# Placing the small matrix products of the norms in a three-block transformer kernel

## The chip, the cores and the metric

The kernel runs on one core of a Trainium2 chip. The metric is the device time of one execution in microseconds (us), smaller is better. The engines of the core are named as in the profile: PE is TensorE (matrix products, with PEld its weight loads), DVE is VectorE, ACT is ScalarE, POOL is GpSimd, SP issues most DMA transfers. Each engine works off its own instructions in the order in which they stand in its queue, and waits at one until what it needs has been signalled by the others.

## The reference

Three transformer blocks follow one another on one sequence of 512 tokens with 1024 features. The first block has a feed-forward network (FFN), a mixer of spatial gating and attention, and an FFN, all with norms that are modulated by a conditioning vector. The second has an FFN, a mixer with a recurrence and a convolution, and an FFN. The third has two layers of an attention mixer and an FFN. In the first two blocks every sub-layer has a norm ahead of it and another behind it; the third block has only the norms ahead, and a last one.

```
def rmsnorm(x, g):
    y = xf * lax.rsqrt(jnp.mean(xf * xf, axis=-1, keepdims=True) + RMS_EPS)
    return (y * g).astype(x.dtype)
def swiglu_2(x, w_gu, w_down):
    gu = x @ w_gu
    gate, up = gu[..., :D_FF], gu[..., D_FF:]
    return (jax.nn.silu(gate) * up) @ w_down
def second_block(...):
        f = swiglu_2(rmsnorm(x, ffn1_norm_pre[l]), ffn1_w_gu[l], ffn1_w_down[l])
        x = x + 0.5 * rmsnorm(f, ffn1_norm_post[l])
        m = hybrid_mixer_2(rmsnorm(x, mix_norm_pre[l]), w_in[l], ...)
        x = x + rmsnorm(m, mix_norm_post[l])
        f = swiglu_2(rmsnorm(x, ffn2_norm_pre[l]), ffn2_w_gu[l], ffn2_w_down[l])
        x = x + 0.5 * rmsnorm(f, ffn2_norm_post[l])
```

All inputs are float32, and D_FF is 2816.

## The kernel before

The sequence is cut into two halves of 256 tokens, half 0 and half 1. Activations lie with features on the partitions, as 8 tiles of 128 features x 256 tokens. Each half goes through the same phases: f10 (first FFN of the first block), m1 (its mixer), f11 (second FFN), f21, m2, f22 in the second block, m30, f30, m31, f31 in the third, and an end. The halves run side by side on the core, half 1 some microseconds behind half 0, so that one half's products can fill TensorE while the other half's norms and attention steps run on VectorE and ScalarE.

A large product is made of float16 parts: a float32 weight tile of 128 x 1024 arrives by DMA (`st`), ScalarE writes its high part (line 368) and VectorE its low part (line 369) into a slot `wr` of a ring of 12 slots (`RING`), and each 128 x 128 piece is used in three products with the high and low parts of the activations (`hh`). The slots are shared by the halves; a slot comes free when both halves have used it. An FFN has 22 tiles of gate and up products (`pgu`, 48 products each) and 8 tiles of down products (`po`, 66 products each); a mixer begins with projections (`pp`, 24 a tile) and ends with 8 `po` tiles of 24. All products go through one helper, so they all have line 320.

A norm is `rstd_bcast` (line 416) with what stands around it. The sum of squares of each token is collected in `acc` on ScalarE and VectorE (`sumsq`, line 434, for the norm ahead of a phase; lines 496 and 497 in `out_tiles` for the norm behind one). Two small float32 products with `ones`, called `nst`, put the sums on partitions; the trace has four records for them. VectorE makes the reciprocal root in small steps (line 421, and `rsqrt` from line 404) and a diagonal of it, `ndg` (line 426); the product `nbc` of ones with `ndg` (two records) spreads it over the partitions. Behind `nbc`, `prenorm` (line 454) scales and splits the 8 tiles of x into `hh` (lines 480, 446 to 450), which the next phase's products read; `postnorm` (line 473) scales the 8 tiles of the phase's output `y` and adds them to x. In the first two blocks a postnorm and the next prenorm of one half follow one another: nst, nbc, update of x and new squares, nst, nbc, `hh`.

What sets the order: the code gives every instruction a priority, and a scheduler makes each engine's fixed order from it when the kernel is built. The priority is the virtual time of the half (`vt[hf]`, which `adv` moves on with every tile of large products, plus `lag`, which is zero for half 0 and `LAGS[ph]`, 16 to 30 us, for half 1), times 200 a microsecond; a smaller number goes first. `boost(us)` moves what is written inside it ahead by so many virtual microseconds. All of a norm stands in `boost(BOOST["norm"])`, 80 us, so each of its steps goes to its engine's queue about as soon as its operands are there.

```
    def now(hf):
        tc.cur_priority = BASE + int((vt[hf] + lag[hf]) * PER_US)
    def boost(us=None):
        return tc.high_priority(int(us * PER_US))
```

Of the kernel before, what the change touches and what calls it, by code (L numbers as in the profile page):

```python
# [20 lines left out]
D = 1024  # L21
KD = 8
# [8 lines left out]
LATE = 6  # L31
WBS = {"m2_o": 0, "gu22": 0}
WB = 0
CB = 80
PB = 10
SEQ = ("G0 G1 G2 G3 K0 K1 K2 K3 U0 P0 U1 P1 C0 R0 R1 C1 R2 R3 B",
# [15 lines left out]
BASE = 2000000  # L52
PER_US = 200
# [195 lines left out]
def tile_three_blocks(ctx: ExitStack, tc: tile.TileContext, d, col_at, con_at, out, phases=None):  # L249
# [20 lines left out]
    vt = [0.0, 0.0]  # L270
    lag = [0.0, LAGS["f10"]]
# [5 lines left out]
# [4 lines that stand above are left out]
        us = CB if us is None else us  # L281
        return tc.high_priority(int(us * PER_US))
# [15 lines left out]
    def t1k(hf, shape=(128, TH), dt=F32, name="t"):  # L298
        return tmp.tile(list(shape), dt, name=name, tag=f"t{hf}")

    def b8k(hf, shape, dt, name):
        return big.tile(list(shape), dt, name=name, tag=f"b{hf}")
# [7 lines left out]
    def tiny(hf, n, name="n", dt=F32, p=128):  # L310
        return tin.tile([p, n], dt, name=name, tag=f"{name}{hf}")
# [4 lines left out]
    def psmall(hf, shape=(128, 512), dt=F32, name="pq"):  # L316
        return pss.tile(list(shape), dt, name=name, tag=f"sm{hf}")

    def mm(out_, l, r, start=True, stop=True):
        return PE.matmul(out_, lhsT=l, rhs=r, start=start, stop=stop, skip_group_check=True)  # L320
# [12 lines left out]
    ones = cons.tile([128, TH], F32, name="ones")  # L333
    V.memset(ones, 1.0)
    ones1 = ones[:, 0:128]
# [22 lines left out]
    class Weights:  # L358
# [3 lines left out]
        def slot(self, s):  # L362
            if s not in self.have:
                with boost(CB if self.name == "gu10" and s < 3 else WBS.get(self.name, WB)):
                    st = stage.tile([128, 1024], F32, name="st", tag="st")
# [38 lines left out]
    def rsqrt(hf, m, y, p=128):  # L404
        shape = list(m.shape)
        n = int(np.prod(shape[1:]))
        a = t1k(hf, name="rsa") if n > 8 else tin.tile([128, 8], F32, name="rsa", tag=f"rsa{hf}")
        a = a[:shape[0], :n]
        mi, yi = m.bitcast(I32), y.bitcast(I32)
        V.tensor_scalar(yi, mi, -0.5, float(0x5f3759df), op0=OP.mult, op1=OP.add)  # L410
        for _ in range(3):
            V.scalar_tensor_tensor(a, y, -0.5, m, op0=OP.mult, op1=OP.mult)
            V.tensor_tensor(a, a, y, op=OP.mult)
            V.scalar_tensor_tensor(y, a, 1.5, y, op0=OP.add, op1=OP.mult)

    def rstd_bcast(hf, acc, n, eps):
        st = psmall(hf, [128, 2, 2], name="nst")
        for j in range(2):
            mm(st[:, j], acc[:, j * 128:(j + 1) * 128], ones[:, 0:2], start=j == 0)
        m, y = tiny(hf, 2, "nm"), tiny(hf, 2, "ny")  # L420
        V.tensor_scalar(m, st[:, :, 0], 1.0 / n, eps, op0=OP.mult, op1=OP.add)
        rsqrt(hf, m, y)
        bc = psmall(hf, [128, TH], name="nbc")
        dg = tin.tile([128, TH], F32, name="ndg", tag=f"ndg{hf}", bufs=1)
        for j in range(2):
            V.tensor_scalar(dg[:, j * 128:(j + 1) * 128], ident, y[:, j:j + 1], None, op0=OP.mult)
        mm(bc, ones1, dg)
        return bc

    def sumsq(hf, src, n, scale=1.0):  # L430
        acc = t1k(hf, name="acc")
        for k in range(n):
            if k == 0:
                S.activation(acc, src(0), AF.Square, scale=scale)
            else:
                t = t1k(hf, name="sq")
                S.activation(t, src(k), AF.Square, scale=scale)  # L437
                V.tensor_tensor(acc, acc, t, op=OP.add)  # L438
        return acc

    def split(hf, hi, lo, src, scale_col=None, bias_col=None):
        if scale_col is not None:
            S.activation(hi, src, AF.Identity, scale=scale_col)
            V.scalar_tensor_tensor(lo, src, scale_col, hi, op0=OP.mult, op1=OP.subtract)
        elif bias_col is not None:
            S.activation(hi, src, AF.Identity, bias=bias_col)
            V.scalar_tensor_tensor(lo, src, bias_col, hi, op0=OP.add, op1=OP.subtract)
        else:
            S.activation(hi, src, AF.Copy)  # L449
            V.tensor_tensor(lo, src, hi, op=OP.subtract)  # L450

    first = {}

    def prenorm(hf, gcol, bcol=None, ph=None):
        if hf and ph:
            lag[1] = LAGS[ph]
        now(hf)
        with boost(BOOST["norm"]):
            x = xs[hf]
            bc = first.pop(hf, None)  # L460
            if bc is None:
                bc = rstd_bcast(hf, sumsq(hf, lambda k: x[:, k], KD), D, 1e-6)
            hh = b8k(hf, [128, 2, KD, TH], F16, "hh")
            for k in range(KD):
                t = t1k(hf, name="nh")
                V.scalar_tensor_tensor(t, x[:, k], gcol(k), bc, op0=OP.mult, op1=OP.mult)
                split(hf, hh[:, 0, k], hh[:, 1, k], t, bias_col=bcol(k) if bcol else None)
        return hh
# [4 lines left out]
    def postnorm(hf, acc, y, gcol):  # L473
        now(hf)
        with boost(BOOST["norm"]):
            bc = rstd_bcast(hf, acc, D, 1e-6)
            x = xs[hf]
            for k in range(KD):
                t = t1k(hf, name="nh")
                V.scalar_tensor_tensor(t, y(k), gcol(k), bc, op0=OP.mult, op1=OP.mult)  # L480
                V.tensor_tensor(x[:, k], x[:, k], t, op=OP.add)
# [32 lines left out]

    def ffn(hf, gu, dn, pre, bias, post, key):
        hh = prenorm(hf, pre, bias, key)
        acts = []
        for n in range(NF):
# [21 lines left out]
        def y(m):  # L540
            if not yb:
                yb[0] = b8k(hf, [128, KD, TH], F32, "y")
            return yb[0][:, m]
        acc = out_tiles(hf, W(dn), NF, x, y, AS / WS, key)
        postnorm(hf, acc, y, post)


# [191 lines left out]

    def mixer1(hf):  # L740
        hh = prenorm(hf, one_col(gpre, 8), one_col(mod, 24), "m1")
        px = pair(hh)
        if hf == 0:
# [127 lines left out]
        with boost(BOOST["mix"]):  # L871
            mix = b8k(hf, [128, 2, KD, TH], F16, "mix")
            bc = rstd_bcast(hf, sumsq(hf, ua, 4), 512, 1e-6)
            for k in range(4):
                t = t1k(hf, name="nh")
                V.scalar_tensor_tensor(t, ua(k), col("gna", k), bc, op0=OP.mult, op1=OP.mult)
                split(hf, mix[:, 0, k], mix[:, 1, k], t)
            for qt in range(2):
                to_channels(hf, ybs[qt], mix, 4, qt, lambda j: col("gnb", j))
        ys = [m2k(hf, [128, 2, TH], F32, "ym") for _ in range(4)]  # L880
        y = lambda m: ys[m // 2][:, m % 2]
        acc = out_tiles(hf, W("m1_o"), KD, pair(mix), y, 1.0 / WS)
        postnorm(hf, acc, y, one_col(gpost, 8))

    def row_rms(hf, y, n):
# [19 lines left out]

    def mixer2(hf):
        hh = prenorm(hf, lambda k: col("mpre2", k), None, "m2")
        px = pair(hh)
        if hf == 0:
# [361 lines left out]
        y = lambda m: ys[m // 2][:, m % 2]  # L1271
        acc = out_tiles(hf, W("m2_o"), KD, lambda k: (mix[:, k, 0], mix[:, k, 1]), y, 1.0 / WS)
        postnorm(hf, acc, y, lambda k: col("mpost2", k))


# [221 lines left out]
    for ph in phases:  # L1497
        if ph == "ada":
# [12 lines left out]
            for groups, key, n0, n1 in (((2, 3, 4), "f10", 2, NF), ((5, 6, 7), "f10", NF, NF + KD), ((8,), "f11", 2, NF)):  # L1511
                steps = [(g, k) for g in groups for k in range(8)]
                for i, (g, k) in enumerate(steps):
                    n = n0 + i * (n1 - n0) // len(steps)
# [28 lines left out]
```

## Time and profile before

| | us |
|---|---|
| three timed runs | 3427.9, 3428.2, 3434.75 |
| their median | 3428.2 |
| the profiled execution's own time | 3428.03 |
| its span in the trace | 3426.1 |
| TensorE busy in it | 3295.0 (96%) |
| VectorE busy | 2105.7 (61%) |
| ScalarE busy | 1372.9 (40%) |
| mean granted clock of TensorE | 0.983 of full speed |
| DMA queue of the weights, share of 16 engines | 30.9% |

A share of busy time is an average over all phases. A wait of TensorE is the time in which its next instruction stood at the head of its queue and an operand was missing; the view of the waits names the instruction that delivered it last. TensorE's clock has two levels, 2.4 GHz (granted clock 1) and 1.2 GHz (0.5), and the granted clock of a stretch is a mean over it.

### The profile page before, as it was taken

The page shows a single profiled execution, that of the slowest core. Times are in us where ns is not written, and L with a number is a line of the kernel's source. Part 1 is how long each engine was busy: PE and PEld are TensorE (multiplying, and loading weights), DVE is VectorE, ACT ScalarE, POOL GpSimd, SP SyncE. Part 2 cuts the span into 40 slices and gives each one's busy share as a digit, 9 for nine tenths or more (in the row PEclk, how much of TensorE's full clock was granted, in tenths as well). Part 3 has the DMA queues.
Part 4 walks back from the last instruction along what each step waited for, and adds up shares of the span by engine and source line. Part 5 has one row for each costly group of instructions (what it writes and reads, how often), then busy time and mean ns, then how long its engine had stood idle before and what let it go on. Part 6 is the DMA issues. An engine that isn't in the chain of part 4 may idle for free.

```text
span 3426.1 us, 71629 instructions
## 1 busy us (share of the span) xinstructions
PE 3295.0 (96%) x30113; PEld 2794.9 (82%) x30120; DVE 2105.7 (61%) x5012; ACT 1372.9 (40%) x2881; POOL 18.7 (1%) x24
## 2 busy tenths in 40 slices
PE   8999999999999999998879999999999999999998
PEld 5888867788888888886658888777888877778887
DVE  8952758844374436598894436996544379845443
ACT  4232356433243324434243334565433255553331
POOL 0000000000000000000000000000000000000000
PEclk9999999999999999997889999999999999999999
DMA  8932434233323333201022333332233343213331
GB/s 307 316 112 87 140 92 133 68 101 103 99 87 99 103 102 106 75 8 35 2 81 99 99 100 125 98 99 82 87 99 108 99 127 121 87 62 106 105 99 44
DMA packets 143603, 351.46 MB, mean 103 GB/s; under 512 B 16808, under 2 KB 58152, under 8 KB 143024
## 3 DMA queue, kind: packets, MB, share of 16 engines
q1 hardware_dynamic: 143280, 346.89, 30.9%
q8 instruction: 235, 3.85, 0.5%
q14 instruction: 88, 0.72, 0.1%
HBM read 334.24 MB, written 12.58 MB: 101 GB/s over the span
## 4 chain that ended last, share of the span: by engine, by line
PE 77%; DVE 15%; ACT 4%; issue 2%; DMA 2%; ACTq 0%; SPq 0%; DVEq 0%
PE pgu L320 38%; PE po L320 20%; PE pp L320 5%; PE ps L320 4%; DVE wr L369 2%; PE pt L320 2%; DVE mix L989 2%; PE ps L659 1%; ACT wr L368 1%; PE pT L320 1%; PE pxy L320 1%; PE pgl L320 1%; DVE acc L438 1%; PE pw L320 1%; DVE nh L480 1%
## 5 line engine op out<-in xcount | busy, mean ns | idle before, releaser
L320 PEld LDWEIGHTS <-wr 128*128 128x128 f16 x24000 | 2348.1, 98 | 326.5 <-issue 26.5
L320 PE MATMUL pgu<-hh,wr 128*128 128x256 f16 x12672 | 1404.7, 273 | 8.4 <-DVE fac L531 2.3
L369 DVE SCALAR_TENSOR_TENSOR wr<-st,wr 128x1024 f16<-128x1024 f32 x524 | 640.0, 1222 | 352.6 <-ACT wr L368 344.1
L320 PE MATMUL po<-act,wr 128*128 128x256 f16 x6336 | 702.0, 273 | 0.1
L368 ACT ACTIVATE wr<-st 128x1024 f16<-128x1024 f32 x524 | 551.5, 1054 | 351.1 <-PE pgu L320 127.3
L320 PE MATMUL pp<-hh,wr 128*128 128x256 f16 x3072 | 377.9, 273 | 3.4 <-DVE rot L1313 1.4
L528 ACT ACTIVATE fth<-pgu 128x256 f32<-128x256 f32 x264 | 100.9, 382 | 573.6 <-PE pgu L320 573.4
L529 DVE SCALAR_TENSOR_TENSOR fth<-fth,pgu 128x256 f32<-128x256 f32 x264 | 110.8, 420 | 349.9 <-ACT fth L528 349.8
L320 PE MATMUL po<-mix,wr 128*128 128x256 f16 x1536 | 195.1, 282 | 17.6 <-DVE wr L369 9.8
L449 ACT ACTIVATE act<-fac 128x256 f16<-128x256 f32 x264 | 109.8, 416 | 185.7 <-DVE fac L531 185.5
L320 PE MATMUL pt<-wr,hh 128*128 128x512 f16 x576 | 141.4, 380 | 1.0 <-DVE wr L369 0.7
L450 DVE TENSOR_TENSOR act<-fac,act 128x256 f16<-128x256 f32 x264 | 111.2, 421 | 48.7 <-ACT act L449 48.3
L497 DVE TENSOR_TENSOR acc<-acc,sq 128x256 f32<-128x256 f32 x84 | 35.3, 420 | 150.2 <-ACT sq L496 150.2
L531 DVE SCALAR_TENSOR_TENSOR fac<-fth,pgu 128x256 f32<-128x256 f32 x264 | 110.7, 419 | 7.7
L437 ACT ACTIVATE sq<-x 128x256 f32<-128x256 f32 x154 | 55.7, 409 | 135.5 <-DVE x L506 130.0
L490 ACT ACTIVATE y<-po 128x256 f32<-128x256 f32 x64 | 24.4, 382 | 203.9 <-PE po L320 203.8
L320 PEld LDWEIGHTS <-hh 128*128 128x128 f16 x768 | 61.5, 99 | 50.4 <-issue 2.8
L647 DVE TENSOR_REDUCE amx<-ps 128x1 f32<-128x128 f32 (+3 forms) x160 | 76.8, 486 | 41.3 <-PE ps L320 36.4
L989 DVE SCALAR_TENSOR_TENSOR mix<-glu,cols,mix 128x256 f32<-128x256 f32 x240 | 101.8, 473 | 0.1
L652 ACT ACTIVATE prob<-ps,amx 128x128 f32<-128x128 f32 (+3 forms) x160 | 84.0, 526 | 35.3 <-DVE amx L647 32.9
L506 DVE SCALAR_TENSOR_TENSOR x<-po,x 128x256 f32<-128x256 f32 x64 | 27.0, 422 | 110.8 <-PE po L320 110.8
L438 DVE TENSOR_TENSOR acc<-acc,sq 128x256 f32<-128x256 f32 x166 | 69.7, 420 | 21.6 <-ACT sq L437 19.2
(357 smaller groups left out, 2727.0 us busy)
## 6 DMA issues: line engine op xcount, KB each, us to landing
st<-in_gu_dram SPq DMA_DIRECT2D x264, 512.0 KB, 3.5
st<-in_dn_dram SPq DMA_DIRECT2D x132, 512.0 KB, 3.5
adw<-in_w_ada_dram SPq DMA_DIRECT2D x112, 256.0 KB, 5.4
st<-in_m_o_dram SPq DMA_DIRECT2D x32, 512.0 KB, 3.6
hd<-heads SPq DMA_DIRECT2D x160, 64.0 KB, 2.0
adr<-in_w_ada_dram SPq DMA_DIRECT2D x16, 512.0 KB, 10.2
st<-in_m_b_dram SPq DMA_DIRECT2D x16, 512.0 KB, 3.9
st<-in_m_a_dram SPq DMA_DIRECT2D x16, 512.0 KB, 3.5
```

The costliest lines, as they stand in the source:

```text
L320: return PE.matmul(out_, lhsT=l, rhs=r, start=start, stop=stop, skip_group_check=True)
L368: S.activation(r[:, 0], st, AF.Copy, scale=WS)
L369: V.scalar_tensor_tensor(r[:, 1], st, WS, r[:, 0], op0=OP.mult, op1=OP.subtract)
L438: V.tensor_tensor(acc, acc, t, op=OP.add)
L449: S.activation(hi, src, AF.Copy)
L450: V.tensor_tensor(lo, src, hi, op=OP.subtract)
L528: S.activation(t, p[:, 0], AF.Tanh, scale=0.5 / WS)
L529: V.scalar_tensor_tensor(t, t, 1.0, p[:, 0], op0=OP.add, op1=OP.mult)
L531: V.scalar_tensor_tensor(a, t, 0.5 / WS / WS / AS, p[:, 1], op0=OP.mult, op1=OP.mult)
L647: V.tensor_reduce(nm, s[:, :nk], axis=AX.X, op=OP.max, negate=True)
L652: S.activation(p[:, :nk], s[:, :nk], AF.Exp, bias=nm, scale=scale, accum_out=sm)
L989: V.scalar_tensor_tensor(cc(j), gl[:, i:i + TH], dw[:, j * 31 + i:j * 31 + i + 1], cc(j), op0=OP.mult, op1=OP.add)
```

## The change

`placed(hf, us)` is a new context. Inside it the priority is set to the half's virtual time plus `us`, whatever boost stands around it. In `rstd_bcast` the two `nst` products are written in `placed(hf, at[0])` and the `nbc` product in `placed(hf, at[1])`; the other steps of the norm keep the boost. Every postnorm uses `NORM_AT` = (4, 8). The prenorm that follows a postnorm in the same half uses `SECOND_AT` = (17, 21) (the dictionary `chain` tells it), and other prenorms use `NORM_AT`. The norms inside the mixers, the very first prenorm and the last norms of the kernel call `rstd_bcast` without `at` and stay as they were; so 31 of 38 norms are placed. No instruction is added or removed.

```diff
--- before.py
+++ after.py
@@ -31,6 +31,8 @@
 LATE = 6
 WBS = {"m2_o": 0, "gu22": 0}
 WB = 0
+NORM_AT = (4, 8)
+SECOND_AT = (17, 21)
 CB = 80
 PB = 10
 SEQ = ("G0 G1 G2 G3 K0 K1 K2 K3 U0 P0 U1 P1 C0 R0 R1 C1 R2 R3 B",
@@ -413,10 +415,19 @@
             V.tensor_tensor(a, a, y, op=OP.mult)
             V.scalar_tensor_tensor(y, a, 1.5, y, op0=OP.add, op1=OP.mult)
 
-    def rstd_bcast(hf, acc, n, eps):
+    @contextmanager
+    def placed(hf, us):
+        saved = tc.cur_priority
+        if us is not None:
+            tc.cur_priority = BASE + int((vt[hf] + lag[hf] + us) * PER_US)
+        yield
+        tc.cur_priority = saved
+
+    def rstd_bcast(hf, acc, n, eps, at=(None, None)):
         st = psmall(hf, [128, 2, 2], name="nst")
-        for j in range(2):
-            mm(st[:, j], acc[:, j * 128:(j + 1) * 128], ones[:, 0:2], start=j == 0)
+        with placed(hf, at[0]):
+            for j in range(2):
+                mm(st[:, j], acc[:, j * 128:(j + 1) * 128], ones[:, 0:2], start=j == 0)
         m, y = tiny(hf, 2, "nm"), tiny(hf, 2, "ny")
         V.tensor_scalar(m, st[:, :, 0], 1.0 / n, eps, op0=OP.mult, op1=OP.add)
         rsqrt(hf, m, y)
@@ -424,7 +435,8 @@
         dg = tin.tile([128, TH], F32, name="ndg", tag=f"ndg{hf}", bufs=1)
         for j in range(2):
             V.tensor_scalar(dg[:, j * 128:(j + 1) * 128], ident, y[:, j:j + 1], None, op0=OP.mult)
-        mm(bc, ones1, dg)
+        with placed(hf, at[1]):
+            mm(bc, ones1, dg)
         return bc
 
     def sumsq(hf, src, n, scale=1.0):
@@ -449,7 +461,7 @@
             S.activation(hi, src, AF.Copy)
             V.tensor_tensor(lo, src, hi, op=OP.subtract)
 
-    first = {}
+    first, chain = {}, {}
 
     def prenorm(hf, gcol, bcol=None, ph=None):
         if hf and ph:
@@ -459,7 +471,7 @@
             x = xs[hf]
             bc = first.pop(hf, None)
             if bc is None:
-                bc = rstd_bcast(hf, sumsq(hf, lambda k: x[:, k], KD), D, 1e-6)
+                bc = rstd_bcast(hf, sumsq(hf, lambda k: x[:, k], KD), D, 1e-6, chain.pop(hf, NORM_AT))
             hh = b8k(hf, [128, 2, KD, TH], F16, "hh")
             for k in range(KD):
                 t = t1k(hf, name="nh")
@@ -473,7 +485,8 @@
     def postnorm(hf, acc, y, gcol):
         now(hf)
         with boost(BOOST["norm"]):
-            bc = rstd_bcast(hf, acc, D, 1e-6)
+            bc = rstd_bcast(hf, acc, D, 1e-6, NORM_AT)
+            chain[hf] = SECOND_AT
             x = xs[hf]
             for k in range(KD):
                 t = t1k(hf, name="nh")
```

On TensorE at the end of f11, where both halves go on to f21: of half 0, nst_10096 and nbc_10113 belong to the postnorm, nst_12102 and nbc_12119 to the next prenorm; nst_12031 and nbc_12048 are half 1's postnorm. po_11747 and po_11889 are half 1's down products and pgu_12158 is a tile of half 0's f21. Before:

```order
L320 MATMUL nst_10096<-ones_96,acc_9502 128x2 x2
...
L320 MATMUL nbc_10113<-ndg_10114,ones_96 128x256
...
L320 MATMUL po_11747<-act_10785,wr_9789 128x256
...
L320 MATMUL nst_12102<-ones_96,acc_12079 128x2 x2
...
L320 MATMUL nbc_12119<-ndg_12120,ones_96 128x256
...
L320 MATMUL po_11889<-act_11350,wr_10002 128x256
...
L320 MATMUL nst_12031<-ones_96,acc_11532 128x2 x2
...
L320 MATMUL pgu_12158<-hh_12124,wr_12161 128x256
...
L320 MATMUL nbc_12048<-ndg_12049,ones_96 128x256
```

115 po stand between nbc_10113 and nst_12102, and 47 between nst_12102 and nbc_12119; half 1's postnorm comes among half 0's pgu. With the change:

```order
L322 MATMUL nst_10096<-ones_96,acc_9502 128x2 x2
...
L322 MATMUL nbc_10113<-ndg_10114,ones_96 128x256
...
L322 MATMUL po_11960<-act_10220,wr_10002 128x256
...
L322 MATMUL po_11960<-act_11350,wr_10065 128x256
L322 MATMUL nst_12031<-ones_96,acc_11532 128x2 x2
L322 MATMUL nst_12102<-ones_96,acc_12079 128x2 x2
L322 MATMUL nbc_12048<-ndg_12049,ones_96 128x256
L322 MATMUL nbc_12119<-ndg_12120,ones_96 128x256
...
L322 MATMUL pgu_12158<-hh_12124,wr_12161 128x256
```

Behind nbc_10113 are 66 po of half 1, its last; then the four small products of both halves stand together, ahead of the first pgu.

On TensorE at the beginning of m2, half 1: nst_16233 and nbc_16250 belong to its postnorm, nst_19009 and nbc_19026 to the prenorm behind it; pp of hh_16324 are half 0's projections, those of hh_19031 half 1's, and nbc_16319 is half 0's prenorm. Before:

```order
L320 MATMUL nst_16233<-ones_96,acc_15734 128x2 x2
...
L320 MATMUL pp_16381<-hh_16324,wr_16384 128x256
...
L320 MATMUL nbc_16250<-ndg_16251,ones_96 128x256
...
L320 MATMUL pp_16454<-hh_16324,wr_16457 128x256
...
L320 MATMUL nst_19009<-ones_96,acc_18986 128x2 x2
...
L320 MATMUL nbc_19026<-ndg_19027,ones_96 128x256
...
L320 MATMUL pp_16600<-hh_16324,wr_16603 128x256
```

32, 87 and 27 of half 0's pp stand in the three gaps between half 1's four small products. With the change:

```order
L322 MATMUL nst_16233<-ones_96,acc_15734 128x2 x2
L322 MATMUL nbc_16319<-ndg_16320,ones_96 128x256
...
L322 MATMUL pp_16381<-hh_16324,wr_16384 128x256
...
L322 MATMUL pp_16783<-hh_16324,wr_16786 128x256
L322 MATMUL nbc_16250<-ndg_16251,ones_96 128x256
L322 MATMUL nst_19009<-ones_96,acc_18986 128x2 x2
L322 MATMUL nbc_19026<-ndg_19027,ones_96 128x256
...
L322 MATMUL pp_19064<-hh_19031,wr_16384 128x256
...
L322 MATMUL pp_19095<-hh_19031,wr_16421 128x256
```

All 288 of half 0's pp (12 tiles) that come before half 1's stand between nst_16233 and nbc_16250; nbc_16250, nst_19009, nbc_19026 and half 1's first pp follow with nothing between them.

## Rows read from the trace of the kernel before

**Rows 1.** Of the page: span, busy time by engine, chain that ended last
```profile
span 3426.1 us, 71629 instructions
...
PE 3295.0 (96%) x30113; PEld 2794.9 (82%) x30120; DVE 2105.7 (61%) x5012; ACT 1372.9 (40%) x2881; POOL 18.7 (1%) x24
...
PE 77%; DVE 15%; ACT 4%; issue 2%; DMA 2%; ACTq 0%; SPq 0%; DVEq 0%
```

**Rows 2.** The stretches' view: us, each engine's busy us, PEclk, DMA share, GB/s
```profile
800.00:950.00 150.00, 150.00 (x1377) 134.44 (x1375) 55.10 (x80) 46.24 (x76) 0.00 (x0) 1.00 0.30 99
```

**Rows 3.** TensorE's waits by cause: us in total, times, longest us
```profile
PE nbc L320 <- DVE ndg L426: 22.3, 32, 2.7
...
PE nst L320 <- DVE acc L438: 11.9, 17, 2.1
...
PE nst L320 <- DVE acc L497: 5.4, 6, 2.9
...
PE pgu L320 <- DVE fac L531: 2.3, 2, 2.0
```

**Rows 4.** The stretches' view, first, fourth and sum of ten phase ends
```profile
41.00:73.00 32.00, 30.70 (x277) 26.98 (x276) 29.65 (x68) 18.58 (x34) 0.00 (x0) 1.00 0.81 269
...
957.00:1030.00 73.00, 68.13 (x587) 58.28 (x585) 58.34 (x162) 30.89 (x66) 0.00 (x0) 0.98 0.24 80
...
sum 526.00, PE 491.74 PEld 421.52 DVE 439.38 ACT 246.35 POOL 9.24; mean PE 49.17 PEld 42.15 DVE 43.94 ACT 24.64 POOL 0.92
```

**Rows 5.** TensorE in order of time at f11's end: start, us, instruction, [idle before]
```profile
958.67 0.61 PE L320 MATMUL nst<-ones,acc 128*128 128x2 f32 x4
...
962.01 0.70 PE L320 MATMUL nbc<-ndg,ones 128*128 128x256 f32 x2 [0.42 <-DVE ndg L426]
962.55 12.72 PE L320 MATMUL po<-act,wr 128*128 128x256 f16 x115
975.92 0.58 PE L320 MATMUL nst<-ones,acc 128*128 128x2 f32 x4 [0.66 <-DVE acc L438]
...
983.60 0.70 PE L320 MATMUL nbc<-ndg,ones 128*128 128x256 f32 x2 [1.95 <-DVE ndg L426]
984.13 9.58 PE L320 MATMUL po<-act,wr 128*128 128x256 f16 x71
993.55 2.02 PE L320 MATMUL pgu<-hh,wr 128*128 128x256 f16 x17
995.86 0.61 PE L320 MATMUL nst<-ones,acc 128*128 128x2 f32 x4 [0.29 <-DVE acc L497]
...
1000.22 0.70 PE L320 MATMUL nbc<-ndg,ones 128*128 128x256 f32 x2 [0.45 <-DVE ndg L426]
...
1012.18 0.58 PE L320 MATMUL nst<-ones,acc 128*128 128x2 f32 x4 [0.67 <-DVE acc L438]
```

**Rows 6.** The same view, half 1's postnorm at the beginning of m2
```profile
1356.26 0.70 PE L320 MATMUL nbc<-ndg,ones 128*128 128x256 f32 x2 [0.51 <-DVE ndg L426]
1356.80 9.66 PE L320 MATMUL pp<-hh,wr 128*128 128x256 f16 x87
1367.09 0.58 PE L320 MATMUL nst<-ones,acc 128*128 128x2 f32 x4 [0.63 <-DVE rkv L960]
```

**Rows 7.** The same view, half 1's norm at the beginning of f30
```profile
2448.68 0.58 PE L320 MATMUL nst<-ones,acc 128*128 128x2 f32 x4 [0.32 <-DVE acc L438]
...
2451.99 0.70 PE L320 MATMUL nbc<-ndg,ones 128*128 128x256 f32 x2 [0.42 <-DVE ndg L426]
...
2453.90 8.33 PE L320 MATMUL pgu<-hh,wr 128*128 128x256 f16 x69 [0.78 <-ACT hh L449]
```

**Rows 8.** The stretches' view, right behind the wait at 983.60
```profile
984.00:988.00 4.00, 4.00 (x23) 2.78 (x22) 3.67 (x10) 1.99 (x6) 0.00 (x0) 0.57 0.51 165
```

**Rows 9.** TensorE in order of time at the end of f22
```profile
2114.90 0.70 PE L320 MATMUL nbc<-ndg,ones 128*128 128x256 f32 x2 [1.27 <-DVE ndg L426]
2115.43 7.92 PE L320 MATMUL po<-act,wr 128*128 128x256 f16 x71
```

## The prediction

> **What bounds the kernel now.** I read the totals first. TensorE is busy for 3295.0 of 3426.1 us and carries 77% of the chain that ended last [rows 1], so every microsecond in which it waits is in the time: 131 us of waits in all. In the middle of a feed-forward phase there is nothing to win, since a stretch of 150 us is wholly busy [rows 2]. Next, the waits of TensorE by cause. The norms' small products account for 22.3 us (nbc, 32 waits), 11.9 and 5.4 us (nst, 23 waits), together 39.6 us [rows 3]; this is all that a better place of these products could give back, 1.2% of the time. Then the ten stretches in which one phase ends and the next begins, 526 us with TensorE busy for 491.74: 34.3 us of waits, the norms' and some others [rows 4]. Last, one such stretch in order of time [rows 5], to see what lies between two small products. There the phase f11 of half 0 has ended, and half 1's last down-products (po, 115 and 47 and 71 of them) run between half 0's four small products; then half 0's first products of f21 (pgu) run between half 1's. Each waits for 0.3 to 2.0 us only, because the other half's work fills what the norm needs on VectorE and ScalarE.
>
> **The lengths that count.** A postnorm's nbc lets 8 rows of x be updated and squared, after which the prenorm's nst can run: 13.9 us from 962.01 to 975.92 for half 0 [rows 5], and 10.8 us from 1356.26 to 1367.09 for half 1, 12.0 us at 1000.22 [rows 5, 6]. The longer ones have weight conversions of VectorE among them. From nst to its own nbc lie 3.3 us and from nbc to the first product that reads the new hh 1.9 us [rows 7]. From half 1's last down-product, at 993.55, to its postnorm's nst pass 2.3 us [rows 5]. An f16 product takes 150 us / 1377 = 0.109 us [rows 2], so 48 take 5.2, 66 take 7.2 and 132 take 14.4. nst itself is busy for 0.6 us and nbc for 0.7 [rows 5].
>
> **The change, part by part.** No instruction is added or taken away; VectorE's and ScalarE's steps of a norm keep their boost. 31 of the 38 norms get new places for nst and nbc on TensorE's queue, which is worked off in order. A product that waits there holds back all behind it. So the question at each place is whether as much work stands between a small product and the next as the chain between them needs. I take the counts from the order of the changed kernel.
>
> *Half 0, feed-forward to mixer or feed-forward.* f11 to f21: behind nbc stand only half 1's last 66 po (7.2 us), then half 1's nst, half 0's nst, both nbc, and only then pgu. The prenorm's nst needs 13.9 us from nbc, then 3.3 to the first nbc; the second norm's steps share VectorE with it, between 0 and 3.3 us more, and I take 2.2 as most of it overlaps nothing else; then 1.9. That is 13.9 + 5.5 + 1.9 = 21.3 us, of which 7.2 are po and 2.6 small products: 11.5 us idle. f22 to the third block's mixer has the same pattern: 11.5. f10 to m1 leaves 132 po behind nbc (14.4, enough), but then the same four products: 2.3 + 5.5 + 1.9 - 2.6 = 7.1. f21 to m2 and m1 to f11 wait for one nbc alone: 2.3 + 4.0 (one chain of 3.3 and a little of the other) - 1.9 = 4.4 each. m2 to f22: 2.5.
>
> *Half 1.* f21 to m2 and m2 to f22: half 1's postnorm nbc is put behind all of half 0's 288 products of the next phase, and behind it come at once the prenorm's nst and nbc and half 1's first products, with nothing between them. Where 87 pp cover the first chain today, now 10.8 - 0.7, 3.3 - 0.6 and 1.9 - 0.7 us are bare: 14.0 each. Half 0 can't fill them: the ring of 12 weight slots is shared, and its slots are only released by half 1's products. m1 to f11 has 48 pgu in the first gap: 14.0 - 5.2 = 8.8. f11 to f21, and half 1's beginning of f30 and f31, have nst and nbc back to back: 2.7 + 1.2 = 3.9 each. f10 to m1: 1.5. f22 to the mixer: the chain of 14 us has some 120 short products in it: 4.5. f30 to m31 keeps 66 products between: 0.2.
>
> *The first phase, half 1.* nst now stands before 8 products of the conditioning rows and right behind comes nbc. The trace has no such row. The bounds are 3 us (the bare 3.9, partly hidden) and 14 us (a whole chain, since VectorE is busy for 29.65 of 32 us there [rows 4]); I take 9, the middle, as VectorE's queue is nearer to the second.
>
> The sum of waits: 9 + (7.1 + 1.5) + (4.4 + 8.8) + (11.5 + 3.9) + (4.4 + 14.0) + (2.5 + 14.0) + (11.5 + 4.5) + 3.9 + 0.2 + 3.9 = 105.1 us. Of the 34.3 us of before some 6 belong to other causes than these norms and stay, so 28 go: +77 us.
>
> *The clock.* Right after the wait of 1.95 us at 983.60 the granted clock of 984 to 988 is 0.57, near the lower of its two levels, 1.2 GHz; the 71 po there take 9.58 us, and 71 po at another phase's end, after 1.27 us, 7.92 [rows 5, 8, 9]. The difference is 1.7 us. I count 13 waits of over 2 us that are new (one in each half at most ends, two where two chains are bare): 13 x 1.7 = +22 us; the least is 5, were it only paid after the longest, the most 40 (3 us after each). The Trainium skill's page "TensorE: Matmul & The Clock Gate" has a rule that speaks against this change, "HAM oscillation — how this bites in real kernels": products in short bursts with waits between them pay the slow restart each time and not once; the trace agrees for one wait, with 0.57 and 1.7 us [rows 8]. By its Part 1 the ramp is under 1% of a typical span, which by an estimate is 34 us at most here. By the first the clock's term stays at 22 us; paid once only, it would be 2 and the sum 3507.
>
> What hides what: VectorE's conversions of weights for the next phase lie in these waits now and might be a cover. They end when the ring is full, and no product stands ready for them, so they give nothing back; but without them half 0's 13.9 us can shrink to 10.8, 3 us less at two ends.
>
> Against the profiled execution's own 3428.03 us (span 3426.1, so 1.9 around it; the median of the runs, 3428.2, is 0.2 from it): 3428.2 + 77 + 22 = 3527.
>
> **The rivals.**
> *Hidden waits, faster.* The new places give the chains time, and the waits of rows 3 vanish: 3428 - 34 to 40 = 3389 to 3394. It decides where the work between nbc and the next nst reaches the chain's 10.8 to 13.9 us, as between nst and nbc at the end of f30, where 66 products of 7.2 us cover a chain of 3.3. For it: the waits of now are short, so that few products more would hide them. Against: at nine of ten ends the work moved is what stood between the small products, which now stand together.
> *Clock unmoved, chains shorter.* The clock falls only where it does today, and half 0's chains take 10.8: 77 - 6 + 5 = +66 at half 0's second-chain share of 2.2; without that share, which stands at two to three ends, and with 3 us in the first phase, +66 - 7 - 6 = +53. That is 3481 to 3494. For it: 1.27 us at 2114.90 did not lower the clock [rows 9]. Against: most new waits are longer than the one that did.
> *More than the chains.* VectorE works in order too. Half 1's rows that wait for a late nbc hold up what stands behind them, half 0's products of the activations, so each long wait drags a second one after it, and the clock stays low for longer. With another 3 us at each of the 13 and 3 us of clock: +77 + 39 + 39 = 3583. For it: pgu products have waited up to 2.0 us for fac, VectorE's, before [rows 3]. Against: the bulk of every phase has the same order as before.
> *Nothing moves.* If the scheduler gave the small products their old turns, the time would stay at 3428. The order of the changed kernel speaks against it at every end.
>
> **How the numbers follow.** The sum, 3500 to 3560: 0.66. Short waits, 3481 to 3500: 0.15. More than the chains, 3560 to 3590: 0.13. Hidden waits: 0.02. Nothing moves or within 0.2% by a balance: 0.02. Dearer or something unseen: 0.02. The likeliest gives 3527; the range from 3488 to 3580 leaves out some 0.2. A measurement of this kernel can tell 0.2% (7 us) from no change: faster 0.02, same 0.02, slower 0.96.
>
> **What would show it.** Right: TensorE's waits of nst and nbc, 39.6 us, grow to over 100, with single waits of over 9 us for VectorE's acc before nst; busy time of the products at the ends grows by some 22 us of low clock; the stretches inside the phases keep their time. Two waits of some 14 us (in two or three pieces) stand at the beginnings of m2 and f22 in half 1, and 66 po followed by about 11 us idle at f11's end. Wrong: nst and nbc with waits below 1 us, other work between them, or a slower bulk of a phase.

## The result: 3.4% slower

| | before | changed |
|---|---|---|
| median of the timed runs, us | 3428.05 (3418.05 to 3434.75) | 3544.43 (3537.53 to 3551.68) |
| ratio, 95% interval | | 1.0336 [1.0318, 1.0354] |
| span of the profiled execution, us | 3426.1 | 3541.3 |
| TensorE busy, us | 3295.0 | 3333.3 |
| TensorE waiting, us (span less busy) | 131.1 | 208.0 |
| mean granted clock | 0.983 | 0.961 |

The time is 116 us more; forecast were 99, within 3488 to 3580. The changed kernel's page, with its span, its busy time, the clock in 40 slices and the chain that ended last, answers to [rows 1]:

```profile
span 3541.3 us, 71617 instructions
PE 3333.3 (94%) x30120; PEld 2825.6 (80%) x30120; DVE 2106.9 (59%) x5012; ACT 1379.9 (39%) x2881; POOL 18.7 (1%) x24
...
PEclk8999999899999999997979999899999999999999
...
PE 81%; DVE 12%; ACT 3%; DMA 2%; issue 1%; SPq 0%; DVEq 0%; ACTq 0%
```

The 115.2 us of span divide into 76.9 us of new waits and 38.3 us in which TensorE is busy for longer with the same products. VectorE and ScalarE are busy for about as long as before (2106.9 against 2105.7 us, 1379.9 against 1372.9).

TensorE's waits by cause, in the columns of [rows 3] (us in total, times, longest):

```profile
PE nbc L322 <- DVE ndg L437: 46.9, 18, 4.7
PE nst L322 <- DVE acc L450: 30.0, 7, 10.1
PE nst L322 <- DVE acc L510: 18.8, 6, 4.8
...
PE pp L322 <- DVE rot L1326: 9.4, 6, 3.8
...
PE pgu L322 <- ACT hh L461: 5.5, 6, 1.0
PE nst L322 <- DVE rsa L414: 4.4, 2, 2.2
```

The small products wait less often than before and far longer each time: nst waited 11.9 us in 17 pieces for `acc` of a prenorm, now 30.0 in 7, one of them 10.1 us. The four rows of nst and nbc make 100.1 us, where [rows 3] had 39.6; over 100 was a sign that the prediction named. In order of time, TensorE has 33 waits of over 2 us, 10 before.

Half 1's norms at the beginning of m2, in order of time on TensorE (the answer to [rows 6]; start, us, instruction, idle before):

```profile
1394.95 1.01 PE L322 MATMUL nst<-ones,acc 128*128 128x2 f32 x4 [3.21 <-DVE acc L510]
1399.83 1.22 PE L322 MATMUL nbc<-ndg,ones 128*128 128x256 f32 x2 [3.87 <-DVE ndg L437]
1402.07 34.81 PE L322 MATMUL pp<-hh,wr 128*128 128x256 f16 x288 [1.02 <-ACT hh L461]
1436.72 0.60 PE L322 MATMUL nbc<-ndg,ones 128*128 128x256 f32 x2
1446.93 0.99 PE L322 MATMUL nst<-ones,acc 128*128 128x2 f32 x4 [9.61 <-DVE acc L450]
1450.65 1.22 PE L322 MATMUL nbc<-ndg,ones 128*128 128x256 f32 x2 [2.73 <-DVE ndg L437]
1452.89 9.32 PE L322 MATMUL pp<-hh,wr 128*128 128x256 f16 x68 [1.02 <-ACT hh L461]
```

From 1436.72 to 1446.93 lie 10.2 us, the 10.8 of [rows 6] with nothing to fill them, where 87 pp stood before. 9.61 + 2.73 + 1.02 = 13.4 us bare. The 68 products behind them take 0.137 us each and not 0.109: that is the clock.

The end of f11, the answer to [rows 5]:

```profile
1014.37 0.60 PE L322 MATMUL nbc<-ndg,ones 128*128 128x256 f32 x2
1014.80 7.37 PE L322 MATMUL po<-act,wr 128*128 128x256 f16 x66
1025.34 0.58 PE L322 MATMUL nst<-ones,acc 128*128 128x2 f32 x4 [3.17 <-DVE acc L510]
1028.13 0.99 PE L322 MATMUL nst<-ones,acc 128*128 128x2 f32 x4 [2.21 <-DVE rsa L414]
1031.40 2.08 PE L322 MATMUL nbc<-ndg,ones 128*128 128x256 f32 x4 [2.29 <-DVE ndg L437]
1034.50 34.15 PE L322 MATMUL pgu<-hh,wr 128*128 128x256 f16 x288 [1.02 <-ACT hh L461]
...
1072.38 0.70 PE L322 MATMUL nbc<-ndg,ones 128*128 128x256 f32 x2 [3.40 <-DVE ndg L437]
```

After 66 po the four small products stand in a row: from nbc at 1014.37 to the second nst at 1028.13 are 13.8 us, the chain of before, with 7.2 us of work in it. 3.17 + 2.21 + 2.29 + 1.02 = 8.7 us are bare, and 3.40 + 1.02 = 4.4 in half 1.

Where it went, end by end. I cut both traces at instructions that stand at the same place of TensorE's order in both, one in the middle of each phase, and added up the idle times that the timeline shows between two cuts. Shown are the new waits, and the rest of the longer time (busy), in us; the last column is the forecast, the term of the sum less the waits of before (70.8 us in all; the forecast added 6 for waits of other causes).

| end of | new waits | longer busy | forecast of waits |
|---|---|---|---|
| first phase, half 1 | 9.8 | 4.6 | 7.7 |
| f10 | 1.6 | 4.0 | 3.7 |
| m1 | 10.3 | 4.9 | 6.2 |
| f11 | 8.4 | 2.8 | 10.5 |
| f21 | 17.7 | 5.2 | 14.2 |
| m2 | 14.3 | 6.3 | 14.2 |
| f22 | 8.1 | 4.2 | 10.8 |
| m30 | 3.3 | 3.2 | 2.3 |
| f30 | 1.5 | 2.4 | -1.0 |
| m31 | 1.9 | 0.6 | 2.3 |

The first column makes 76.9, the second 38.2. The middles of the phases keep their time: nothing but the ends moved.

The clock, from the view of stretches of the changed kernel (us, busy us of each engine, PEclk, DMA): the end of f21 with two stretches of its products apart, half 1's bare wait at m2, the products behind it, and the middle of a phase:

```profile
1394.00:1408.00 14.00, 8.07 (x33) 5.47 (x34) 11.13 (x45) 4.27 (x9) 0.00 (x0) 0.52 0.30 104
1402.00:1408.00 6.00, 5.84 (x27) 3.88 (x27) 5.24 (x15) 2.82 (x8) 0.00 (x0) 0.50 0.00 1
1408.00:1411.00 3.00, 3.00 (x28) 2.53 (x26) 0.00 (x0) 0.88 (x3) 0.00 (x0) 0.98 0.00 0
1436.00:1453.00 17.00, 3.64 (x18) 2.54 (x16) 12.58 (x43) 4.48 (x12) 0.00 (x0) 0.68 0.00 0
1453.00:1456.00 3.00, 2.92 (x14) 1.86 (x13) 3.00 (x10) 1.82 (x5) 0.00 (x0) 0.51 0.00 0
1456.00:1466.00 10.00, 10.00 (x93) 8.84 (x91) 7.05 (x16) 6.91 (x15) 0.00 (x0) 1.00 0.25 71
800.00:830.00 30.00, 30.00 (x277) 26.89 (x276) 14.49 (x24) 9.75 (x17) 0.00 (x0) 1.00 0.33 106
```

At 0.5 the clock is at its lower level. At the end of f21 it is there from about the end of the first wait (3.21 us, until 1394.95), through the two other waits (3.87 and 1.02 us) and for 6 us of products behind them. At m2 it falls within the wait of 9.61 us and is back 3 us behind the last one. With a mean of 0.961 it stood there for 2 x 0.039 = 7.8% of the span, 276 us, and for 2 x 0.017 x 3426 = 116 us before.

### The profile page after: what moved, and what is told of

Read it like the earlier page. It is cut to its first block, busy times and chain, and to the rows that moved or that the text cites. A ratio compares the mean times of both kernels' runs of the same rounds, so it can differ in the third digit from the quotient of the medians.

```text
span 3541.3 us, 71617 instructions
## 1 busy us (share of the span) xinstructions
PE 3333.3 (94%) x30120; PEld 2825.6 (80%) x30120; DVE 2106.9 (59%) x5012; ACT 1379.9 (39%) x2881; POOL 18.7 (1%) x24
## 4 chain that ended last, share of the span: by engine, by line
PE 81%; DVE 12%; ACT 3%; DMA 2%; issue 1%; SPq 0%; DVEq 0%; ACTq 0%
PE pgu L322 38%; PE po L322 21%; PE pp L322 8%; PE ps L322 4%; PE pt L322 2%; DVE mix L1002 2%; DVE wr L371 1%; PE ps L672 1%; PE pxy L322 1%; PE pw L322 1%; PE pgl L322 1%; DMA st<-in_gu_dram 1%; DVE nh L493 1%; DVE acc L450 1%; PE pT L322 1%
## 5 line engine op out<-in xcount | busy, mean ns | idle before, releaser
L322 PE MATMUL pp<-hh,wr 128*128 128x256 f16 x3072 | 390.6, 280 | 14.8 <-DVE rot L1326 9.4
L322 PE MATMUL po<-mix,wr 128*128 128x256 f16 x1536 | 190.5, 279 | 17.6 <-DVE wr L371 10.1
## 6 DMA issues: line engine op xcount, KB each, us to landing
adr<-in_w_ada_dram SPq DMA_DIRECT2D x16, 512.0 KB, 10.2
```

## The experiments

Theory 1 is the prediction's: a wait is the length of the chain between two small products less the work that the order leaves between them, and the clock takes a share on top. To put numbers on it, I walked through each kernel's order on TensorE with the lengths of the prediction (13.9 and 10.8 us from nbc to the next nst, 3.3 from nst to nbc, 1.9 to the first product, 2.2 from the last po) and added up what stays bare. For the changed kernel that is 64 us more than for the one before.

### Only the postnorms, only the prenorms (e1, e2)

```diff
-                bc = rstd_bcast(hf, sumsq(...), D, 1e-6, chain.pop(hf, NORM_AT))
+                bc = rstd_bcast(hf, sumsq(...), D, 1e-6, (None, None))
```

> Only the 12 postnorms are placed; every prenorm keeps its boost. Theory 1 (each new wait is the length of the chain between two small products less the work that the order leaves between them, and about half as much again is lost to TensorE's clock): counted in this kernel's order, the two bare chains of some 10 us in half 1 at the beginnings of m2 and f22 stay, and one more of that kind comes at the beginning of m1, since a boosted prenorm behind a late postnorm is just as bare. Waits +61 us, time about +110: 3539 us. Theory 2 (each placed norm costs its own share, whatever stands around it: 116 us / 31 = 3.7 us): 12 x 3.7 = +45, 3473 us.

Measured: 3500.71 us, ratio 1.0206 [1.0171, 1.0242]. Span 3499.2, waits +49 us (180.0 against 131.1), busy +24. The bare chain that theory 1 expected at the beginning of m1 didn't come: half 1's nst there waited 0.69 us, at 458.27, because half 0's attention steps, which wait for other engines themselves, take longer than the products that I had counted between (one of them waited 5.24 us there, at 455.69).

The second kernel takes the place from the postnorms instead:

```diff
-            bc = rstd_bcast(hf, acc, D, 1e-6, NORM_AT)
+            bc = rstd_bcast(hf, acc, D, 1e-6)
```

> Only the 19 prenorms are placed; every postnorm keeps its boost. Theory 1: the long chain from a postnorm's nbc to the prenorm's nst is covered again by the other half's products, and what stays bare is nst to nbc and nbc to the first product, 2.7 + 1.2 us at seven ends. Waits +30 us, time about +54: 3482 us; no wait of nst for acc of over 3 us in half 1. Theory 2 (3.7 us a norm): 19 x 3.7 = +71, 3499 us.

Measured: 3504.45 us, ratio 1.0217 [1.0181, 1.0254]. Span 3504.2, waits +45, busy +34. The first kernel's total lies between the two theories. This one's is above both, 5 us from theory 2 and 22 from theory 1, whose count of +30 us was too low. So the totals don't speak for theory 1; the places do. With only the prenorms placed, half 1 at the beginning of m2:

```profile
1397.66 0.70 PE L322 MATMUL nbc<-ndg,ones 128*128 128x256 f32 x2
1398.20 24.29 PE L322 MATMUL pp<-hh,wr 128*128 128x256 f16 x221
1422.33 0.51 PE L322 MATMUL nst<-ones,acc 128*128 128x2 f32 x4
1425.83 1.22 PE L322 MATMUL nbc<-ndg,ones 128*128 128x256 f32 x2 [3.00 <-DVE ndg L437]
1428.07 12.15 PE L322 MATMUL pp<-hh,wr 128*128 128x256 f16 x87 [1.02 <-ACT hh L461]
```

221 products stand in the long chain, and nst doesn't wait at all; the short chains stay bare with 3.00 and 1.02 us. Over the whole kernel, nst's longest wait for `acc` of a prenorm is 2.1 us here, and 10.1 with only the postnorms placed. So the long wait is the late postnorm's, the 4 us the prenorm's, as theory 1 has it. The two halves of the change don't add up: 49 + 45 us of waits against 77 for both.

### Only half 0, only half 1 (e3, e4)

```diff
-        if us is not None:
+        if us is not None and hf == 0:
```

> Only half 0's norms are placed. Theory 1: half 0's pattern at the ends of f11 and f22 (66 po, then four small products together) stays, half 1 has its covered chains back. Waits +14 us, time about +25: 3453 us. Theory 2 (3.7 us a norm, about half of the norms): +58, 3486 us.

Measured: 3466.09 us, ratio 1.0108 [1.0071, 1.0145]; waits +29, busy +11. The time lies between the theories, 13 us above theory 1 and 20 below theory 2; the waits are twice the count. Of the busy time, 6.5 us less than before come from the recurrence of m2, where no norm was moved (the last section has more on it); without it busy would be +17.

The second kernel has `hf == 1` in the same place:

> Only half 1's norms are placed. Theory 1: half 1's bare chains stay, and since half 0 goes on early, its products ahead of half 1's norm have run out at more ends: bare chains of some 10 us at the beginnings of f21 and m30 too. Waits +85 us, time about +150: 3580 us, slower than the whole change. Theory 2 (3.7 us a norm, about half of them): +58, 3486 us.

Measured: 3545.26 us, ratio 1.0335 [1.0291, 1.0378]; waits +84.5 us (215.6), busy +36. Theory 2 is out: it has both at 3486, and they lie 79 us apart, half 1 alone as slow as the whole change. The waits of theory 1 came as counted in this kernel, the bare chain at the beginning of f21 too, which the change itself doesn't have there:

```profile
1060.56 0.60 PE L322 MATMUL nbc<-ndg,ones 128*128 128x256 f32 x2
1071.27 0.99 PE L322 MATMUL nst<-ones,acc 128*128 128x2 f32 x4 [10.11 <-DVE acc L450]
1074.99 1.22 PE L322 MATMUL nbc<-ndg,ones 128*128 128x256 f32 x2 [2.73 <-DVE ndg L437]
```

What was too high in theory 1 here is the factor of 1.8 by which I turned counted waits into time: 120 us of span came of 85. Of the four kernels so far, the count itself came out only in this one: it was 61 for 49 and 30 for 45 above, and 14 for 29 with half 0 alone.

### Filling the waits (e5)

```diff
         with placed(hf, at[0]):
+            if n1:
+                mm(ps_[:, 256:512], ones1, late, stop=False)
+            for i in range(n1):
+                mm(ps_[:, 256:512], identb, mk2, start=False, stop=i == n1 - 1)
             for j in range(2):
                 mm(st[:, j], acc[:, j * 128:(j + 1) * 128], ones[:, 0:2], start=j == 0)
...
         with placed(hf, at[1]):
+            if n2:
+                mm(pb_[:, 256:258], ones1, m, stop=False)
+            for i in range(n2):
+                mm(pb_[:, 256:512], identb, mk2, start=False, stop=i == n2 - 1)
             mm(bc, ones1, dg)
```

`n1` and `n2` are the numbers of filling products, up to 74 and 24 at eight of the placed norms and none at the others. `late` is the first tile of the updated x, or a late tile of y, so that the filling begins with the chain and not before.

> The whole change, with 352 extra products of constants (0.11 us each, about 39 us, into unused columns of the small products' PSUM tiles, their results are never read) in the order just where TensorE waits for a norm in after: half 1's norms at the beginnings of f11, f21, m2 and f22, and both halves' at the ends of f11 and f22. They start only when the chain itself is under way and end before it does, so they fill waits and lengthen none. Theory A (what is lost beside the waits is the low clock that follows them): waits fall by about 38 us, the half-clock time falls from 282 us by 60 or more, and the time falls by 12 to 23 us, to 3521 to 3532 us. Theory B (the products are slower for another reason, so that filling a wait changes nothing): the time stays at 3544, or grows by a few us.

Measured: 3533.11 us (3529.85 to 3536.96), 11 us under the changed kernel's 3544.43; ratio to before 1.0308 [1.0283, 1.0333]. Waits 170.0 us, 38 fewer, as meant. TensorE is busy for 3357.8 us, 24.5 more, though the filling is 44.0 us of it; the kernel's own products, with the few that start the filling, got shorter by 19.5. The mean clock is 0.972, 198 us at the lower level. Half 1 at the beginning of m2, and the stretches over its wait and behind it:

```profile
1430.69 0.60 PE L324 MATMUL nbc<-ndg,ones 128*128 128x256 f32 x2
...
1433.18 8.24 PE L324 MATMUL nst<-maskb,identb 128*128 128x256 bf16 x74
1441.26 0.51 PE L324 MATMUL nst<-ones,acc 128*128 128x2 f32 x4
...
1442.26 2.12 PE L324 MATMUL nbc<-maskb,identb 128*128 128x256 bf16 x18
1444.50 0.70 PE L324 MATMUL nbc<-ndg,ones 128*128 128x256 f32 x2
...
1446.89 18.32 PE L324 MATMUL pp<-hh,wr 128*128 128x256 f16 x162 [0.29 <-DVE hh L479]
```

```profile
1430.00:1447.00 17.00, 13.93 (x116) 11.47 (x115) 13.22 (x45) 5.10 (x13) 0.00 (x0) 1.00 0.00 1
1447.00:1466.00 19.00, 19.00 (x171) 16.55 (x170) 14.10 (x35) 12.24 (x26) 0.00 (x0) 1.00 0.36 112
```

The chain is about as long as before (10.6 us from nbc to nst, 10.2 in the changed kernel), but the clock stays at 1.00 in it and behind it, and 162 products take 0.113 us each. By cuts as above, some 16 of the 19.5 us lie at the six places that are filled, and 2.3 in the recurrence of m2, where nothing is. So theory A holds in its mechanism: the clock's share is a cost of its own that comes of the waits, since products with no use at all take away 16 of 38 us. The time shows it less well. The gain of 11 us is just under the 12 to 23 that I expected, and the two kernels were timed beside different runs of before: the ratios are 1.0336 and 1.0308, and their intervals overlap. In the trace the six places are only 4 us shorter in all, because the filling with the products that start it takes 48.6 us there, 12 more than the waits that it removes.

### Places in between, and a smaller ring (e6, e7)

```diff
-NORM_AT = (4, 8)
-SECOND_AT = (17, 21)
+NORM_AT = (-10, -8)
+SECOND_AT = (0, 2)
```

> Places 14 to 17 virtual us earlier: NORM_AT (-10, -8), SECOND_AT (0, 2). By the order the bare chains are then partly covered: waits +13 us against before where the change has +64 by the same count. Theory 1: time about +24, 3452 us. Theory 2 (that a norm is placed at all costs 3.7 us, wherever): 3544 us as the change itself.

Measured: 3479.22 us, ratio 1.0153 [1.0125, 1.0181]; waits +35 us, busy +12. The change's cost falls by more than half with the same norms placed, but it is double what I expected. The count left waits out that are not of the small products: projections that wait for VectorE's rotary step (`pp` for `rot`, 6.7 us here, 9.4 in the changed kernel, 1.4 before) and products that wait for `hh` tile by tile.

```diff
-RING = 12
+RING = 10
```

> The whole change with a ring of 10 weight slots in place of 12. If the ring is what stops half 0 while half 1's norm waits, 240 products of half 0's next phase stand ahead of half 1's small products at the beginnings of f21, m2 and f22, not 288, the waits behind them are as long as in after (9.6 us before nst at m2), and more waits come elsewhere: +18 us of waits by the count, 3560 to 3580 us. If it was the priority that put them there, the 288 stay and the time too, but for weights that come later.

Measured: 3614.45 us, ratio 1.054 [1.051, 1.057], above what I expected, since a smaller ring costs in other places too (po waited 17.7 us for weights, 9.8 before). What it was meant to tell is in the order of time at the beginning of m2:

```profile
1457.95 28.56 PE L322 MATMUL pp<-hh,wr 128*128 128x256 f16 x240 [1.02 <-ACT hh L461]
1486.35 0.60 PE L322 MATMUL nbc<-ndg,ones 128*128 128x256 f32 x2
1496.56 0.98 PE L322 MATMUL nst<-ones,acc 128*128 128x2 f32 x4 [9.60 <-DVE acc L450]
```

240 products, ten slots of 24, and the same 9.6 us behind them: half 0 has used up the ring when half 1's norm begins. So the ring, and not the priority, ends half 0's products there and leaves the wait unfilled. A larger ring was not tried.

### Early places, for all norms (e8) or twelve (e9), and one norm by itself (e10)

```diff
-NORM_AT = (4, 8)
-SECOND_AT = (17, 21)
+NORM_AT = (-23, -21)
+SECOND_AT = (-16, -14)
```

> Places well ahead: NORM_AT (-23, -21), SECOND_AT (-16, -14), so that a small product waits at most for the end of the other half's running tile. By the order the waits for norms are 3 us fewer than in the kernel before. Theory 1: 3422 to 3428 us, within or just under the 0.2% that can be told. Rival (the later turns of a few us lengthen the norms' chains and the next phase starts later): 3435 to 3445 us.

Measured in 12 runs: 3441.37 us (3433.44 to 3451.53), ratio 1.004 [1.0024, 1.0057], slower by 0.4%. The waits of nst and nbc are fewer, as counted (29 us against 41 before), but others took their place: 8.2 us of `pp` for `rot`, 5.0 of pgu for `fac` (VectorE's step behind gate and up products), 1.4 and 2.3 before. The rival was right, with its mechanism in another place than I had it: what is late next is VectorE's work, not the next phase's start. The trace shows only part of it: the profiled execution took 3435.89 us, 7.9 more than that of before (4.7 of it waits), where the medians are 14.5 apart.

```diff
+PLACED = {0, 2, 3, 5, 8, 10, 11, 12, 13, 14, 15, 17}
...
+        if at[0] is not None:
+            turn[0] += 1
+            if turn[0] - 1 not in PLACED:
+                at = (None, None)
```

`turn` counts the norms that the change places, in the order in which they are written.

> The early places of e8 (NORM_AT (-23, -21), SECOND_AT (-16, -14)), but only for the twelve norms at the ends of f10, f11 and f21; all others keep their boost. By e8's own trace, cut at instructions that both kernels have at the same place, these three stretches are 0.9, 3.1 and 5.3 us shorter than before and the others 16 longer. If the stretches are independent of one another: 9 us less than before, 0.27%. If e8's 5.3 us at f21's end is a chance of the clock (4.1 of it is no wait): 4 to 5 us less, which can't be told from nothing. If early turns cost what they give: no difference.

Measured in 12 runs: 3427.89 us against 3422.98 in 17 runs of before, ratio 1.0009 [0.9996, 1.0022]: no difference. The waits are 4.2 us fewer in the profiled execution, but at f21's end the clock took 4.4 us where e8's had given 4.1; that part was a chance. In both it lies in the recurrence of m2, which that stretch takes in, and not at the norms. No version here beats the kernel before.

```diff
+PLACED = {1}
...
+            if turn[0] - 1 not in PLACED:
+                at = (None, None)
```

> Only half 1's prenorm of f10, the first norm that the change places, is at (4, 8); all others keep their boost. If the ends add up, the time is that of before plus the 14 us by which this stretch is longer in after (10 us of waits, the rest the clock): 3438 to 3443 us. If the stretch is longer for what comes later in the whole change, or if the lost time is won back in the rest of f10, under 4 us.

Measured: 3444.23 us, ratio 1.0069 [1.0044, 1.0093]; the span is 13.2 us longer than before. By the cuts the stretch to the middle of f10 is 15.1 us longer (9.7 of it waits) and every other stretch is within some 2. So in the trace this end costs by itself what it costs in the whole change (14.4), and nothing is won back behind it. The timed runs give more: 21 us over the 3422.98 of before, 15 to 32 by the interval, against the 14 that I expected; no trace shows where the rest comes from. This is the place that the trace of before had no row for:

```profile
70.48 0.51 PE L323 MATMUL nst<-ones,acc 128*128 128x2 f32 x4
75.24 3.54 PE L323 MATMUL pad<-ones,ada 128*128 128x2 f32 x16 [4.25 <-DVE ada L589]
83.52 1.22 PE L323 MATMUL nbc<-ndg,ones 128*128 128x256 f32 x2 [4.73 <-DVE ndg L442]
86.43 3.79 PE L323 MATMUL pgu<-hh,wr 128*128 128x256 f16 x16 [1.69 <-ACT hh L463]
```

4.25 us for the rows of the conditioning vector, 4.73 for the norm's own chain and 1.69 for `hh`.

## Why the prediction was right, and where it was off

**The waits** were sized at +77 us and came to +77, by ends within some 4 us each. That the sum agrees so well is partly luck: m1 and f21 came 4 us dearer each, f11 and f22 2 to 3 cheaper, and 8 of the measured 77 are waits of a kind that the sum didn't have (below).

**Half 1's bare chains**, 14.0 us by the sum, are 13.4, with the lengths of [rows 5 to 7] as they stood. E4 shows the same chain at one more end, and e2 shows it covered.

**The ring** as the reason that nothing covers them is shown by e7.

**Four small products together** (f11, f22): 11.5 was too high by 2.8. The 2.2 us for the second norm's steps on VectorE didn't come: from the second nst, at 1028.13, to both nbc are 3.3 us, one chain's length. VectorE began the other norm's steps at 1025.95 and ran most of them in turn with this norm's between 1029.15 and 1031.4, at 0.1 to 0.3 us each, and this lengthened nothing. At the ends of f21 it did come: 4.9 us from nst to nbc, where the sum had 4.0.

**The first phase**: 9 us, the middle between 3 and 14, which is 7.7 more than before; 9.8 more were measured. It was a choice without a row; that it came near shows nothing of how to choose.

**The clock** is the term that was mis-sized: 13 x 1.7 = 22 us, measured 38.3. The number of waits failed, and not the price: where the sum counted 13 new waits of over 2 us, about one to a place, there are 23 more than before, since many places have two or three in a row (3.21 and 3.87 us ahead of m2's first products, 9.61 and 2.73 behind the first 288). 38.3 us for 23 waits are 1.7 each, the price read from one wait of 1.95 us [rows 8]. That the average came out so well is partly luck again: at the end of f11 four such waits cost 2.8 us, in the first phase two cost 4.6. The upper bound, 40, just held it. By the Trainium skill's page "TensorE: Matmul & The Clock Gate", "HAM oscillation — how this bites in real kernels", the slow restart is paid with each gap; here the trace agrees, with 5.2 and 6.3 us at the ends of f21 and m2, and e5 shows that it goes when the gap is filled (1.00 over the filled wait at m2). By Part 1 of that page of the Trainium skill the ramp is under 1% of a typical span, by an estimate at most 34 us here; the 38.3 us that this change alone adds are more.

**What the sum left out** is 8 us of projections that wait for VectorE's rotary step, the rival of "more than the chains" in small. They are there in every kernel that moves the norms from f22's end on (8.1 us in all with the prenorms alone, 9.1 with half 0 alone, 1.4 before), and not in e9 and e10, which leave these norms alone. That late norms push VectorE's rotary steps back was not followed step by step. The rival's own example, pgu that waits for `fac`, did not come: 0.8 us, 2.3 before.

**The rivals.** Hidden waits: not here; e8 has the shorter norm waits, and gets nothing for them. Nothing moves: no. Clock unmoved: no. The sum of this last one has a slip: 77 - 6 + 5 is 76 and not 66, so its times would have been 3491 to 3504, still far below the measured 3544. A reading of [rows 5] has one too: the 71 po stand behind half 0's fourth small product, and only the 115 and 47 between them. Neither enters the forecast.

## What to carry to other kernels

- A small product that hands a value on in a long chain through other engines is not cheap to delay: each turn that it loses is lost to the whole chain. Count the work that the order leaves between it and the next link, and compare it with the chain's length; what is missing is a wait.
- Where two streams share a ring of buffers, the one that is ahead can fill the other's wait only as far as the ring goes. Delaying the slower stream's norm until the ring is used up leaves the wait bare.
- When you price the clock, count every wait that a change makes, since a place with two or three waits in a row is not one wait. And check a gain in waits against what else becomes late.

## What was not expected of the hardware

The granted clock fell behind a wait as short as 1.95 us and stayed low for 4 us of products [rows 8]. Behind the last of the longer waits at f21's end and at m2 it is low for 6 and 3 us, no longer by much; what makes the low stretch at the end of f21 14 us long is that it runs on through two more waits.

And it falls with hardly a wait. In the kernel before, in the recurrence of m2 (columns as in [rows 2]):

```profile
1500.00:1541.00 41.00, 40.60 (x756) 34.34 (x754) 38.33 (x95) 11.31 (x24) 0.00 (x0) 1.00 0.04 9
1541.00:1558.00 17.00, 17.00 (x80) 13.97 (x80) 7.68 (x28) 4.50 (x13) 0.00 (x0) 0.50 0.00 1
```

A row of the first stretch, from the view in order of time:

```profile
1533.76 1.15 PE L320 MATMUL pT<-nt,nm 64*64 64x64 f32 x32
```

TensorE was busy for 40.60 of 41 us, much of it with such small float32 products, and then for all of 17 us at half the clock. Why it fell there was not tried. Between 1541 and 1749 the granted clock is 0.79, so most of the 116 us at the lower level before the change lie in this recurrence, some of them behind waits. What it costs differs from one profiled execution to the next, though no norm is moved there: cut out by itself, the recurrence's busy time is between 6.5 us less (e3) and 4.9 us more (e9) than before. That is as much as the early places of e9 were expected to bring.
